# A two-layer encoder: who stores the inverse blocks, when the keys are loaded, and where the post-processing of the recurrence stands

## The chip, the cores and the metric

The kernel runs on one core of a Trainium2 chip. The metric is the device time of one execution in microseconds (us), as the median over runs.

## The reference, cut to what matters

The model has two layers over 1024 positions of width 1024, each a mixer and a SwiGLU feed-forward block with RMS norms and residuals. Layer 0 mixes with a chunked gated MLP beside a pooling mixer. Layer 1 mixes with RWKV-7, a recurrence with a delta rule in 16 heads of 64:

```python
def step(state, inp):
    r_t, w_t, k_t, v_t, a_t, b_t = inp
    sa = jnp.einsum('bhvk,bhk->bhv', state, a_t)
    state = (state * w_t[:, :, None, :] + sa[..., None] * b_t[:, :, None, :]
             + v_t[..., None] * k_t[:, :, None, :])
    return state, jnp.einsum('bhvk,bhk->bhv', state, r_t)
...
mean = jnp.mean(y, axis=-1, keepdims=True)
var = jnp.mean(jnp.square(y - mean), axis=-1, keepdims=True)
y = ((y - mean) * lax.rsqrt(var + GN_EPS)).reshape(bsz, seq, d)
y = y * ln_w.astype(f32) + ln_b.astype(f32)
bonus = jnp.sum(rh * kh * r_k.astype(f32), axis=-1, keepdims=True) * vh
y = (y + bonus.reshape(bsz, seq, d)).astype(h.dtype)
return (y * g) @ w_o, v_first
...
def swiglu(hn, w_gate, w_up, w_down):
    return (jax.nn.silu(hn @ w_gate) * (hn @ w_up)) @ w_down
```

Everything is float32.

## The kernel before

The positions are worked in two halves of 512, called half 0 and half 1 (A and B in the tiles of the stream). A float32 product is done as three products of high and low parts (`mm3`, lines 409 to 411); ScalarE makes the high part (`split`, line 159) and VectorE the low one (line 160). A Tile scheduler sets the order of the instructions on each engine, from the order of the code, from `issue_after` (an instruction that has to be issued behind another) and from a simulated timeline. `drive` interleaves two generators: a stream of dense products (`ffn`, a feed-forward block of a half) and the recurrence, by the numbers that each yields.

For each half, `project` computes the projections of the RWKV mixer and stores keys (`ab_d`), values (`v_d`) and gates (`g_d`) in HBM. The recurrence is done in eight chunks of 64 positions; each chunk needs the inverse of a triangular matrix per head, whose 32x32 diagonal blocks are inverted ahead of it, in `project`. This is `invert` (line 1432), run twice for a half: GpSimd clears the tile `xi` (line 1437), VectorE copies the diagonal (line 1438) and does 31 pairs of a product and a sum (lines 1443 and 1448), makes a transposed copy (line 1450), and three transfers store the blocks to `xi_d` (lines 1452 and 1454). The tile has one buffer, so that the clearing of the second inverse waits for the three stores of the first.

`recur` (line 1469) is the recurrence of a half. `load(c)` (line 1504) loads chunk c: keys `ar` from `ab_d`, the blocks `XT` from `xi_d`, the values `uv` from `v_d`, all on SyncE's queue. The start is `load(0)`, then a stream of other loads, then `load(1)`. `gram` makes the first products of a chunk from the keys (`sm<-ar`), which VectorE turns into `gt`; `flip_bk` transposes keys (`sm<-ident,ar`); `below` and `below2` solve with `XT` and `gt`; `own` solves the chunk's own part into `uv`. `burst(c)` is what a chunk does once the state is there: `below2`, `own`, the next chunk's `gram`, the output `yp`, copied to `ysb` by ScalarE, then the next chunk's transposes, the load of the chunk after it, and its `below`.

`post(jj)` is the post-processing of two chunks, in pieces: loads of gates `gch` and values `vch`, statistics (`bn_stats`), the normalisation, and the gain and bonus on `ysb` (lines 1713 and 1714). It is made after each odd burst, and `between` runs one more of its pieces at three places of a burst. `turn_out`, in the even burst, has TensorE transpose `ysb`, VectorE multiply by the gate (`gch`, line 1731) and SyncE store the result to `y_d`.

For half 0 the main program then opens a tile pool `y0` where the recurrence's memory (`wp0`) was and loads `y_d` into the stream tiles `ahi` and `alo` (`open_act`, `take_act`; ScalarE issues the load of `raw`, then splits it), which the output projection reads. Beside it runs the last group of half B's down projection (`steps_b`), whose sums VectorE adds to the residual `h` (line 503).

```python
ps_es = open_psum("psm0", MIXED)
hb_pool, hb_es = open_pool(name="hb1", bufs=1, side="left")
wp, wp_es = open_pool(name="wp0", bufs=1, side="left")
...
drive(ffn(0, 1, nxt["hn"], f, D0P[:3], nd=2), recur(0, wp, in_pieces(hb_pool, 1, h_d[1, 0]), 6.2), 6.2)
wp_es.close()
y, y_es = open_pool(name="y0", bufs=1, side="left")
ys = open_act(("y", 0), y)
between.append(with_first(0))
drive(ffn(0, 1, nxt["hn"], f, D0P[3:], nd=2))
drive(steps_b)
```

Of the kernel before, what the change touches and what calls it, by code (L numbers as in the profile page):

```python
# [16 lines left out]
P = 128  # L17
# [28 lines left out]
def tile_trunk(  # L46
# [29 lines left out]
    def open_pool(**kw):  # L76
        es = ExitStack()
        pl = es.enter_context(tc.tile_pool(reuse_waits="tile", **kw))
        return pl if kw["name"].startswith("wp") else Lines(pl), es
# [301 lines left out]
    def open_psum(name, tags):  # L381
        es = ExitStack()
        pl = es.enter_context(tc.tile_pool(name=name, bufs=1, space=PSUM, reuse_waits="tile"))
        psum["pool"], psum["tags"] = pl, tags
        return es
# [27 lines left out]
    def rsqrt(t):  # L413
        pool.tensor_tensor(out=t, in0=t, in1=mhalf[:, : t.shape[1]], op=ALU.pow)
# [46 lines left out]
        return norm_bcast(norm_sums(h))  # L461

    def act_tiles(pool_, n=HT):
        return [pool_.tile([P, KT, n], F32R, tag=t, name=t) for t in ("ahi", "alo")]

    def norm_split(h, c0, pool_, spill=None, b=None):

# [964 lines left out]
    def invert(h, p0, iat, tmp):  # L1432

        x2 = tmp("xi", 1, [P, 32, 2, 32])
        xi = x2[:, :, 1, :]
        xf = x2.rearrange("p i a c -> p (i a c)")
        pool.memset(xf, 0.0)
        dve.tensor_copy(xf[:, 32:2048:65], iat[:, 31, :])
        for j in range(31):
            n = 31 - j  # L1440
            t = tmp("it", 1, [P, 256])[:, : n * (j + 1)].rearrange("p (i c) -> p i c", c=j + 1)
            sh = [P, n, j + 1]
            dve.tensor_tensor(  # L1443
                out=t, in0=bc(iat[:, j, j + 1 : 32].unsqueeze(2), sh), in1=bc(xi[:, j, 0 : j + 1].unsqueeze(1), sh),
                op=ALU.mult,
            )
            xs = xi[:, j + 1 : 32, 0 : j + 1]
            dve.tensor_tensor(out=xs, in0=xs, in1=t, op=ALU.add)
            yield
        dve.tensor_copy(x2[:, :, 0, :], xi.rearrange("p i c -> p c i"))  # L1450
        to = xi_d[h][p0 : p0 + 4].rearrange("p r c q i x -> (p r c) q i x")
        sp.dma_start(to[:, 0, :, 0:64], x2[0:64].rearrange("s i a j -> s i (a j)"))
        for q in range(2):
            sp.dma_start(to[:, q, :, 64 - 32 * q : 96 - 32 * q], x2[64:128, :, 0, :])  # L1454

# [11 lines left out]
    def recur(h, wp, stream, ratio):  # L1469
# [5 lines left out]
        def wt(tag, bufs, shape):  # L1475
            return wp.tile(shape, F32, tag=tag, bufs=bufs, name=tag)
# [27 lines left out]
        def load(c):  # L1504
            ab = wt("ar", 2, [P, 2, 8, 2, 64])
            sp.dma_start(ab, ab_d[h][c])
            ar, bk = ab[:, 0], ab[:, 1]
            XT = wt("XT", 2, [P, 8, 96])
            for r in range(2):
                sp.dma_start(XT[rows[r]], xi_d[h][:, r ^ (c % 2), c].rearrange("p q i x -> (q i) p x"))  # L1510
            uv = wt("uv", 2, [P, 2, 8, 64])
            vs = v_d[h][c * 64 : c * 64 + 64]
            sp.dma_start(uv[64:128, 0], vs[:, 0])
            loaded[0] = sp.dma_start(uv[0:64, 1], vs[:, 1])
            gt = wt("gt", 2, [P, 8, 2, P])
            C[c] = (ar, bk, uv, gt, XT)

        def gram(c, q):
            ar, bk, _, gt, _ = C[c]
# [69 lines left out]
        def burst(c, bkt, w1):  # L1589

            ar, _, uv, gt, XT = C[c]
            cg, S0, more = h * 8 + c, S[0], c < 7
            below2(c, w1)
            between()
            Q = own(c, S0)
            between()
            yield 0.1
            if more:
                gram(c + 1, 0)
                between()  # L1600
                yield 0.1
            ou = smt()
            yp = psum["pool"].tile([P, 8, 64], F32, tag="y", bufs=1, name="yp")
            for p in range(8):
                for r in range(2):
                    mm(ou[rows[r], p, :], XT[rows[r], p, 0:64], Q[rows[r], p, :], start=True, stop=True)
                    mm(
                        yp[rows[1 - r], p, :], ar[rows[r], p, 1, :], S0[rows[r], p, :], start=p == 0, stop=False,
                        skip_group_check=True,
                    )  # L1610
            act.activation(uv[rows[0], 0], ou[rows[0]], AF.Copy)
            chain[0] = dve.tensor_copy(uv[rows[1], 1], ou[rows[1]]).ins
            between()
            yield 0.1
            if more:
                gram(c + 1, 1)
                between()
                yield 0.1
            if cg < NCH - 1:
                Sn = wt("S", 2, [P, 8, 64])  # L1620
                os_ = smt()
                each(os_, lambda r, p: bkt[:, p, r * 64 : r * 64 + 64], lambda r, p: uv[:, r, p, :])
                tS = wt("Q", 1, [P, 8, 64])
                dve.tensor_tensor(out=tS, in0=S0, in1=os_, op=ALU.add)
                chain[0] = dve.tensor_tensor(out=Sn, in0=tS, in1=bc(pct[:, cg, :].unsqueeze(2), [P, 8, 64]), op=ALU.mult)
                chain[0] = chain[0].ins
                S[0] = Sn
                between()
                if c == 7:
                    sp.dma_start(state_d, Sn)  # L1630
                yield 0.1
            for p in range(8):
                for r in range(2):
                    mm(
                        yp[rows[1 - r], p, :], gt[:, p, r, 64:128], uv[:, r, p, :], start=False, stop=p == 7,
                        skip_group_check=True,
                    )
            ysb = wt("ysb", 3, [P, 8, 64])
            act.activation(ysb, yp, AF.Copy)
            ypair.append(ysb)  # L1640
            C.pop(c)
            yield 0.1
            if more:
                bkt = flip_bk(c + 1)
                if turned or pieces:
                    for _ in pieces.pop():
                        pass
                    turned.pop()()
                if c < 6:
                    load(c + 2)  # L1650
                if c == 0:
                    with tc.issue_after(loaded[0].ins):
                        for r in range(2):
                            i = sp.dma_start(
                                lnw[rows[1 - r]],
                                rwkv_ln_w[0].rearrange("(p r d) -> r p d", r=2, d=64)[r].partition_broadcast(64),
                            )
                    loaded.append(i)
                yield 0.1
                w1 = below(c + 1)  # L1660
                yield 0.1
            return bkt, w1

        turned, chain, pieces = [], [None], []

        def between():
            if pieces:
                with tc.issue_after(chain[0]):
                    next(pieces[0], None)

        def post(jj):
            ysb = [ypair.pop(0) for _ in range(2)]
            j = h * 4 + jj
            gch = wt("gch", 1, [P, 8, P])
            vch = wt("vch", 1, [P, 2, 8, 64])
# [10 lines left out]
            st = wt("st", 1, [P, 2, 8, 6])  # L1686
            yield
            for r in range(2):
                for p in range(8):
                    dve.bn_stats(out=st[:, r, p, :], in_=ysb[r][:, p, :])  # L1690
                yield
# [7 lines left out]
            dve.tensor_tensor(out=var, in0=var, in1=dm, op=ALU.add)  # L1699
            dve.tensor_scalar(out=var, in0=var, scalar1=1.0 / 64, scalar2=GN_EPS, op0=ALU.mult, op1=ALU.add)  # L1700
            rsqrt(var)
            yield
            dve.scalar_tensor_tensor(out=mean, in0=mean, scalar=-0.5, in1=var, op0=ALU.mult, op1=ALU.mult)
            vb, mb = (bc(t[:, 0:8].unsqueeze(2), [P, 8, 64]) for t in (var, mean))
# [36 lines left out]
        with tc.issue_after(loaded[0].ins):  # L1741
            stream_loaded = stream()
        with tc.issue_after(stream_loaded):
            load(1)
        yield START * ratio
        last.append(newest[0])
# [5 lines left out]
        w1 = below(0)  # L1752
        yield 2.0
        for c in range(8):
            bkt, w1 = yield from burst(c, bkt, w1)
            yield BURST / 2
            if c % 2 == 1:
                pieces[:] = [post(c // 2)]
                next(pieces[0])
            yield BURST / 2  # L1760
        for _ in pieces[0]:
            yield 0.3
        turned.pop()()
# [223 lines left out]


    ps_es = open_psum("psm0", MIXED)
    hb_pool, hb_es = open_pool(name="hb1", bufs=1, side="left")  # L1990
    wp, wp_es = open_pool(name="wp0", bufs=1, side="left")
    f, f_es = open_pool(name="ffn1", bufs=1, side="right")
# [5 lines left out]
    drive(ffn(0, 1, nxt["hn"], f, D0P[:3], nd=2), recur(0, wp, in_pieces(hb_pool, 1, h_d[1, 0]), 6.2), 6.2)  # L1998
    wp_es.close()
    y, y_es = open_pool(name="y0", bufs=1, side="left")  # L2000
    ys = open_act(("y", 0), y)
    between.append(with_first(0))
    drive(ffn(0, 1, nxt["hn"], f, D0P[3:], nd=2))
    drive(steps_b)
# [26 lines left out]
        yield from ffn(1, 0, hnA, f, G1A[0], nd=2, after=spill_a)  # L2031

    def norm_a():
        hnA.extend(norm_split(0, C_FFN + 8, y, n_d[1], norm_bcast(sums)))

    beside(1, blocks(), [1] * 8 + weights_of(G1A[0]), parts, (8, norm_a))
    for e in (f_es, y_es, hb_es, ps_es):
        e.close()
    ps_es = open_psum("psp1", PROJ)
    project(1, hn1, kp, ring, keep, early("n1", "act2", nxt["a_es"]))  # L2040
# [70 lines left out]
```

## Time and profile before

| | before |
|---|---|
| median of 3 runs | 2402.95 us (2401.16 to 2412.61) |
| profiled execution, its own time | 2407.23 us |
| its span | 2405.5 us |
| TensorE busy | 2319.2 us, 96% |
| VectorE, ScalarE, GpSimd busy | 1464.6, 946.9, 171.2 us |
| granted TensorE clock, mean | 0.986 |

The profiled execution is one run, with a profiler on; its span runs from the first to the last instruction. PE is TensorE's matrix products, PEld its weight loads, DVE VectorE, ACT ScalarE, POOL GpSimd, SP SyncE, and SPq or ACTq the issue of a DMA on that engine's queue. A row of waits gives total us, number and longest. A row of a timeline gives start, length, engine, line, operation, the tile written and those read, and in brackets how long the engine had been idle and what ended it. Line numbers are those of the kernel before, unless the text says otherwise. Half 0's recurrence begins near 1043 us and ends near 1240, half 1's runs from about 1600 to 1790.

### The profile page before, as it was taken

Reading aid. Unit: us, or ns where it says so; the run is one execution under the profiler, and the core shown is the slowest. Engines: PE = TensorE matmul, PEld = TensorE weight load, DVE = VectorE, ACT = ScalarE, POOL = GpSimd, SP = SyncE. Lnnn points to the kernel's source line nnn. Section 1 sums busy time; section 2 is a strip of 40 time slices with the busy share of each in tenths; the row PEclk is TensorE's granted clock in tenths of the full one; section 3 lists DMA queues with packets and bytes.
Section 4 is the critical chain, followed back from the end, with each engine's and each line's share of the span. In section 5 each row is a group of like instructions: output and inputs, shape, how many; then the busy total and the mean of one; then the engine's idle time right before and its main releaser. Section 6 shows DMA issues by size and latency. Waiting matters only on the chain.

```text
span 2405.5 us, 37578 instructions
## 1 busy us (share of the span) xinstructions
PE 2319.2 (96%) x15315; PEld 1893.9 (79%) x15315; DVE 1464.6 (61%) x2312; ACT 946.9 (39%) x1467; POOL 171.2 (7%) x195
## 2 busy tenths in 40 slices
PE   8999999999999999889899999998999999999998
PEld 6888888888888788667777777777778788888886
DVE  6445775665568858656768958765664546444443
ACT  6233444444224755323336665423332225222223
POOL 0200000000000022101100022101010001000001
PEclk9999999999999999999999999999999999999999
DMA  5114472334765565775445475776534433433231
GB/s 181 53 49 145 149 198 83 129 99 146 283 226 191 156 173 140 209 218 157 130 135 165 148 199 147 193 222 177 163 89 149 123 88 119 127 96 97 79 114 44
DMA packets 446157, 347.97 MB, mean 145 GB/s; under 512 B 119776, under 2 KB 393312, under 8 KB 443680
## 3 DMA queue, kind: packets, MB, share of 16 engines
q10 hardware_dynamic: 266048, 195.33, 27.3%
q1 hardware_dynamic: 179936, 150.25, 20.9%
q8 instruction: 120, 1.97, 0.4%
q14 instruction: 53, 0.43, 0.1%
HBM read 266.47 MB, written 79.04 MB: 144 GB/s over the span
## 4 chain that ended last, share of the span: by engine, by line
PE 77%; DVE 9%; DMA 6%; issue 2%; ACT 2%; SPq 2%; POOL 2%; ACTq 0%; POOLq 0%; DVEq 0%
PE mm L409 17%; PE mm L410 17%; PE mm L411 17%; PE mm L740 5%; PE mm L742 5%; PE mm L741 5%; PE sm L1491 3%; DMA ar<-ab_d 1%; DVE wlo L160 1%; DMA raw<-y_d 1%; SPq L1454 1%; DVE it L1443 1%; DMA raw<-in_ffn_w_down_dram 1%; PE mm L590 1%; PE mm L591 1%
## 5 line engine op out<-in xcount | busy, mean ns | idle before, releaser
L409 PE MATMUL mm<-ahi,whi 128*128 128x512 f32 x1376 | 541.0, 394 | 4.2 <-ACT ahi L159 2.6
L410 PE MATMUL mm<-alo,whi 128*128 128x512 f32 x1376 | 542.0, 394 | 0.9 <-DVE alo L160 0.9
L411 PE MATMUL mm<-ahi,wlo 128*128 128x512 f32 x1376 | 540.6, 393 | 1.6 <-DVE wlo L160 1.6
L159 ACT ACTIVATE whi<-raw 128x1024 fp32r<-128x1024 f32 (+2 forms) x284 | 286.3, 1014 | 507.1 <-PE mm L410 367.7
L160 DVE TENSOR_TENSOR wlo<-raw,whi 128x1024 fp32r<-128x1024 f32 (+2 forms) x284 | 337.6, 1192 | 233.6 <-ACT whi L159 212.4
L409 PEld LDWEIGHTS mm<-ahi,whi 128*128 128x128 f32 x1376 | 259.0, 188 | 62.9 <-issue 3.5
L411 PEld LDWEIGHTS mm<-ahi,wlo 128*128 128x128 f32 x1376 | 259.2, 188 | 58.5 <-DVE wlo L160 2.9
L410 PEld LDWEIGHTS mm<-alo,whi 128*128 128x128 f32 x1376 | 259.3, 188 | 57.4 <-issue 2.9
L503 DVE TENSOR_TENSOR h<-h,mm 128x512 f32<-128x512 f32 x276 | 185.9, 684 | 156.1 <-PE mm L411 152.9
L411 PE MATMUL mm<-hidhi,wdlo 128*128 128x512 f32 x304 | 119.6, 394 | 0.0
L409 PE MATMUL mm<-hidhi,wdhi 128*128 128x512 f32 x304 | 117.2, 392 | 2.3 <-ACT sg L957 2.3
L410 PE MATMUL mm<-hidlo,wdhi 128*128 128x512 f32 x304 | 118.6, 390 | 0.0
L740 PE MATMUL mm<-ahi,whi 128*128 128x512 f32 x296 | 115.6, 390 | 0.0
L741 PE MATMUL mm<-alo,whi 128*128 128x512 f32 x296 | 115.2, 389 | 0.0
L742 PE MATMUL mm<-ahi,wlo 128*128 128x512 f32 x296 | 113.6, 389 | 0.0
L965 DVE TENSOR_TENSOR sg<-sg,mm 128x512 f32<-128x512 f32 x52 | 35.7, 686 | 125.7 <-PE mm L411 125.7
L159 ACT ACTIVATE wdhi<-raw 128x1024 fp32r<-128x1024 f32 x42 | 43.6, 1058 | 169.0 <-PE mm L410 126.9
L160 DVE TENSOR_TENSOR wdlo<-raw,wdhi 128x1024 fp32r<-128x1024 f32 x42 | 51.4, 1223 | 30.9 <-ACT wdhi L159 29.2
L409 PEld LDWEIGHTS mm<-hidhi,wdhi 128*128 128x128 f32 x304 | 57.2, 188 | 14.7 <-ACT sg L957 2.7
L411 PEld LDWEIGHTS mm<-hidhi,wdlo 128*128 128x128 f32 x304 | 57.2, 188 | 12.2 <-issue 0.5
L410 PEld LDWEIGHTS mm<-hidlo,wdhi 128*128 128x128 f32 x304 | 57.2, 188 | 12.0 <-issue 0.2
L409 PE MATMUL mm<-xhi,whi 128*128 128x512 f32 (+1 forms) x160 | 64.9, 406 | 0.0
(392 smaller groups left out, 4226.2 us busy)
## 6 DMA issues: line engine op xcount, KB each, us to landing
raw<-in_ffn_w_down_dram ACTq DMA_DIRECT2D x88, 512.0 KB
raw<-in_ffn_w_gate_dram ACTq DMA_DIRECT2D x74, 512.0 KB
raw<-in_ffn_w_up_dram ACTq DMA_DIRECT2D x74, 512.0 KB
hid_d<-hid SPq DMA_DIRECT2D x36, 512.0 KB
ar<-ab_d SPq DMA_DIRECT2D x16, 1024.0 KB
hd<-hid_d SPq DMA_DIRECT2D x26, 512.0 KB
raw<-in_ab_w_in_dram ACTq DMA_DIRECT2D x16, 512.0 KB
raw<-in_ab_w_out_dram ACTq DMA_DIRECT2D x16, 512.0 KB
```

The lines of the kernel that those rows point to most:

```text
L159: act.activation(hi, src, AF.Copy)
L160: (eng or dve).tensor_tensor(out=lo, in0=src, in1=hi.bitcast(F32), op=ALU.subtract)
L409: pe.matmul(o, whi, xhi, start=first, stop=False)
L410: pe.matmul(o, whi, xlo, start=False, stop=False)
L411: newest[0] = pe.matmul(o, wlo, xhi, start=False, stop=last).ins
L503: dve.tensor_tensor(out=H[h][:, m, :], in0=H[h][:, m, :], in1=o, op=ALU.add)
L590: pe.matmul(ops[j], xhi[:, k, sl], whi[:, kk], start=(k == 0), stop=False)
L740: pe.matmul(o, wh[:, k, :], x[0][:, k, :], start=st, stop=False, skip_group_check=True)
L741: pe.matmul(o, wh[:, k, :], x[1][:, k, :], start=False, stop=False, skip_group_check=True)
L742: pe.matmul(o, wl[:, k, :], x[0][:, k, :], start=False, stop=k == 3, skip_group_check=True)
L965: dve.tensor_tensor(out=s, in0=s, in1=o, op=ALU.mult)
L1491: i = f(*args, **kw)
```

## The change

The three stores of an inverse go from SyncE's to GpSimd's queue. `load` no longer loads `XT` for chunk 0; a new `load_x(0)` does it behind the stream's loads, so keys and values are issued first. `post` is begun ahead of the odd burst and takes each `ysb` when its statistics are due; `between` may run one piece of it in the odd burst and any number in the even one, and an extra empty `yield` shifts the normalisation by one place. The stream tile `ahi` of half 0's output gets a pool of its own (`y0hi`), outside the recurrence's memory; `alo` stays.

```diff
     def act_tiles(pool_, n=HT):
-        return [pool_.tile([P, KT, n], F32R, tag=t, name=t) for t in ("ahi", "alo")]
+        return [(pool_[i] if type(pool_) is tuple else pool_).tile([P, KT, n], F32R, tag=t, name=t) for i, t in enumerate(("ahi", "alo"))]
...
         to = xi_d[h][p0 : p0 + 4].rearrange("p r c q i x -> (p r c) q i x")
-        sp.dma_start(to[:, 0, :, 0:64], x2[0:64].rearrange("s i a j -> s i (a j)"))
+        pool.dma_start(to[:, 0, :, 0:64], x2[0:64].rearrange("s i a j -> s i (a j)"))
         for q in range(2):
-            sp.dma_start(to[:, q, :, 64 - 32 * q : 96 - 32 * q], x2[64:128, :, 0, :])
+            pool.dma_start(to[:, q, :, 64 - 32 * q : 96 - 32 * q], x2[64:128, :, 0, :])
...
             ar, bk = ab[:, 0], ab[:, 1]
-            XT = wt("XT", 2, [P, 8, 96])
-            for r in range(2):
-                sp.dma_start(XT[rows[r]], xi_d[h][:, r ^ (c % 2), c].rearrange("p q i x -> (q i) p x"))
             uv = wt("uv", 2, [P, 2, 8, 64])
             vs = v_d[h][c * 64 : c * 64 + 64]
             sp.dma_start(uv[64:128, 0], vs[:, 0])
             loaded[0] = sp.dma_start(uv[0:64, 1], vs[:, 1])
-            gt = wt("gt", 2, [P, 8, 2, P])
-            C[c] = (ar, bk, uv, gt, XT)
+            C[c] = (ar, bk, uv, wt("gt", 2, [P, 8, 2, P]), wt("XT", 2, [P, 8, 96]))
+            if c:
+                load_x(c)
+
+        def load_x(c):
+            for r in range(2):
+                loaded[0] = sp.dma_start(C[c][4][rows[r]], xi_d[h][:, r ^ (c % 2), c].rearrange("p q i x -> (q i) p x"))
...
                 bkt = flip_bk(c + 1)
-                if turned or pieces:
-                    for _ in pieces.pop():
-                        pass
+                if c and c % 2 == 0:
+                    exhaust(pieces.pop())
                     turned.pop()()
...
-        turned, chain, pieces = [], [None], []
+        turned, chain, pieces, open_ = [], [None], [], [0]
 
         def between():
-            if pieces:
+            if pieces and open_[0]:
+                open_[0] -= 1
                 with tc.issue_after(chain[0]):
                     next(pieces[0], None)
 
         def post(jj):
-            ysb = [ypair.pop(0) for _ in range(2)]
+            ysb = []
...
             for r in range(2):
+                ysb.append(ypair.pop(0))
                 for p in range(8):
...
             rsqrt(var)
+            yield
             yield
...
             stream_loaded = stream()
         with tc.issue_after(stream_loaded):
+            load_x(0)
+        with tc.issue_after(loaded[0].ins):
             load(1)
...
         for c in range(8):
-            bkt, w1 = yield from burst(c, bkt, w1)
-            yield BURST / 2
             if c % 2 == 1:
                 pieces[:] = [post(c // 2)]
                 next(pieces[0])
-            yield BURST / 2
+            open_[0] = (99, 1)[c % 2]
+            bkt, w1 = yield from burst(c, bkt, w1)
+            yield BURST
...
+    yhi, yhi_es = open_pool(name="y0hi", bufs=1, side="left")
...
-    ys = open_act(("y", 0), y)
+    ys = open_act(("y", 0), (yhi, y))
...
-        hnA.extend(norm_split(0, C_FFN + 8, y, n_d[1], norm_bcast(sums)))
+        hnA.extend(norm_split(0, C_FFN + 8, (yhi, y), n_d[1], norm_bcast(sums)))
```

Since a scheduler sets the order, the following rows show it, in the order of issue on one engine: line, operation, the tile written and those read, shape, number.

SyncE at the start of half 0's recurrence, before, from the last v_d store on (`waits` names what the transfer waits for: DMAHW a transfer of SyncE or ScalarE, DMASW one of GpSimd, PE, DVE or Pool an engine):

```order
L1425 DMA v_d_1976<-epx 256x1x256 [waits DMAHW4_49,Activation_49]
L1452 DMA xi_d_1982<-xi 64x32x64 [waits DMAHW1_49,DVE_49,Pool_49]
L1454 DMA xi_d_1982<-xi 64x32x32 [waits DMAHW2_49]
L1454 DMA xi_d_1982<-xi 64x32x32 [waits DMAHW3_49]
L1506 DMA ar<-ab_d_1974 128x2048 [waits DMAHW5_49,PE_49]
L1510 DMA XT<-xi_d_1982 64x8x96 [waits DMAHW4_49,DMAHW3_49,DMAHW6_49,DMAHW2_49,DMAHW1_49]
```

After (with the new kernel's line numbers; `h` is the stream of half B's residual):

```order
L1425 DMA v_d_1976<-epx 256x1x256 [waits DMAHW1_49,Activation_49]
L1506 DMA ar<-ab_d_1974 128x2048 [waits DMAHW3_49,DMAHW2_49,DMAHW6_49,DMAHW1_49,DMAHW0_49]
L1510 DMA uv<-v_d_1976 64x512 [waits PE_49]
L1511 DMA uv<-v_d_1976 64x512 [waits DMAHW2_49]
L1848 DMA h<-h_d_86 128x1024 [waits DMAHW4_49,DMAHW3_49,PE_49]
L1518 DMA XT<-xi_d_1982 64x8x96 [waits DMASW3_49,DMASW4_49,DMASW2_49,DMASW5_49,DMASW1_49,DMAHW7_49,DMASW0_49,PE_49]
```

The keys no longer stand behind stores of an inverse; `XT` waits for all six of GpSimd.

TensorE at the same place, before (`hidhi` and `whi` are a dense product of half B's feed-forward block):

```order
L409 MATMUL mm<-hidhi,whi 128x512
L410 MATMUL mm<-hidlo,whi 128x512
L411 MATMUL mm<-hidhi,wlo 128x512
L1491 MATMUL sm<-ar 64x128 x32
L1491 MATMUL sm<-ident,ar 128x128 x8
L1491 MATMUL sm<-XT,gt 32x32 x16
```

After:

```order
L411 MATMUL mm<-hidhi,wlo 128x512
L1491 MATMUL sm<-ar 64x128 x32
L409 MATMUL mm<-hidhi,whi 128x512
L1491 MATMUL sm<-ident,ar 128x128 x8
L410 MATMUL mm<-hidlo,whi 128x512
L411 MATMUL mm<-hidhi,wlo 128x512
```

One dense product stands ahead of the transposes now, and 15 between them and the first use of `XT`; before, none. In half 1 there are 46 dense products from the first keys' product to the first use of `XT`, where there were 29.

GpSimd's queue at the two inverses of half 0, after (before, the first rows are followed by the MEMSET alone):

```order
L1374 TENSOR_SCALAR ar<-kkn 128x8 [waits PE_49,Activation_49]
L1377 TENSOR_TENSOR kkn<-kkn,av 128x512 [waits DMAHW1_49,DMAHW2_49,DMAHW0_49,DMAHW7_49,DVE_49,Pool_49]
L1452 DMA xi_d_1982<-xi 64x32x64 [waits DVE_49]
L1454 DMA xi_d_1982<-xi 64x32x32 x2
L1437 MEMSET xi 128x2048 [waits DMASW2_49,DMASW1_49,DMASW0_49]
L1452 DMA xi_d_1982<-xi 64x32x64 [waits DVE_49,Pool_49]
L1454 DMA xi_d_1982<-xi 64x32x32 x2
L1485 MEMSET S 128x512 [waits DMAHW7_49,DMAHW0_49,Activation_49]
```

The stores stand around the memset of the second inverse, which waits for the first three of them.

ScalarE at the end of half 0's recurrence, before (`ysb` is the last block, `raw<-y_d` the load for the output projection):

```order
L1706 ACTIVATE ysb<-ysb,mean,var 128x64 x8
L123 DMA raw<-in_rwkv_w_o_dram 64x4x128 x3
L159 ACTIVATE whi<-raw 128x1024
L968 ACTIVATE hidhi<-sg 128x512
L123 DMA raw<-y_d_82 128x1024
L159 ACTIVATE ahi<-raw 128x1024
```

After:

```order
L1710 ACTIVATE ysb<-ysb,mean,var 128x64 x8
L159 ACTIVATE whi<-raw 128x1024
L419 ACTIVATE nacc<-h 128x512
L422 ACTIVATE nsq<-h 128x512 x5
L123 DMA raw<-y_d_82 128x1024 x3
L422 ACTIVATE nsq<-h 128x512 x2
L159 ACTIVATE ahi<-raw 128x1024 x2
```

The load of the output stands behind squares of half B's residual (`nacc`, `nsq`), and thus at the end of its down projection. On TensorE the last transposes of `ysb` are followed by 84 dense products of half B before the output projection begins, and by 18 after the change.

More of the change, by code (lines that the diff above doesn't have):

```diff
@@ L2033, in norm_a @@
     def norm_a():
-        hnA.extend(norm_split(0, C_FFN + 8, y, n_d[1], norm_bcast(sums)))
+        hnA.extend(norm_split(0, C_FFN + 8, (yhi, y), n_d[1], norm_bcast(sums)))
     beside(1, blocks(), [1] * 8 + weights_of(G1A[0]), parts, (8, norm_a))
-    for e in (f_es, y_es, hb_es, ps_es):
+    for e in (f_es, y_es, hb_es, yhi_es, ps_es):
         e.close()
```

## The prediction

> **What bounds the kernel now.** I read the page first, for the busiest engine, and then the list of what that engine waited for.
>
> ```profile
> PE 2319.2 (96%) x15315; PEld 1893.9 (79%) x15315; DVE 1464.6 (61%) x2312; ACT 946.9 (39%) x1467; POOL 171.2 (7%) x195
> ```
> ```profile
> PE sm L1491 <- DMA ar<-ab_d: 12.8, 3, 9.5
> ```
>
> TensorE works for 96% of the span, and the change removes no matrix product. It can only win or lose idle time of TensorE, plus what a lowered clock costs behind such a pause. The largest single group of waits is for the keys `ar`, 12.8 us in three waits. The chain that ended last shows how the first of them comes about, at the start of half 0's recurrence:
>
> ```profile
> 1035.34 1.11 DVE xi L1450
> ...
> 1036.50 0.61 SPq L1452
> ...
> 1037.16 2.63 SPq L1454
> ...
> 1039.84 4.50 SPq L1454
> ...
> 1044.43 7.93 DMA ar<-ab_d
> ```
>
> The same chain at the start of half 1:
>
> ```profile
> 1592.46 9.81 DMA ar<-ab_d
> 1602.32 3.04 PE sm L1491 x64
> ```
>
> TensorE's timeline says how long it stood:
>
> ```profile
> 1052.41 3.69 PE L1491 MATMUL sm<-ar 64*64 64x128 f32 x64 [9.50 <-DMA ar<-ab_d]
> ```
>
> The keys themselves had been in HBM for long. What delays them is SyncE's queue, in which the three stores of the second inverse stand ahead of them (SyncE's timeline):
>
> ```profile
> 979.23 0.62 SPq L1452 DMA_DIRECT2D xi_d<-xi  x1
> 979.89 11.28 SPq L1454 DMA_DIRECT2D xi_d<-xi  x2
> 991.27 2.42 SPq L1274 DMA_DIRECT2D iat<-at_d  x1
> ...
> 1017.73 0.84 SPq L1425 DMA_DIRECT2D v_d<-epx  x1
> ```
>
> **A. Keys ahead, half 0.** SyncE's last work before the recurrence is now the v_d store, over at 1018.6. The keys are issued there and have 24 us before TensorE wants them at 1042.9 (1052.41 less 9.50). The first wait goes: -9.5 us. The 64 products took 3.69 us here and 3.04 us in half 1, and the windows show why:
>
> ```profile
> 979.00:991.00 12.00, 10.56 (x47) 8.41 (x46) 3.53 (x3) 2.61 (x3) 0.00 (x0) 1.00 0.92 241
> 991.00:1000.00 9.00, 9.00 (x41) 7.42 (x41) 1.38 (x2) 2.52 (x4) 1.15 (x1) 1.00 1.01 246
> ...
> 1036.00:1049.00 13.00, 6.90 (x31) 5.39 (x29) 3.99 (x5) 2.74 (x4) 0.00 (x0) 0.91 0.97 223
> 1049.00:1060.00 11.00, 7.07 (x201) 6.35 (x201) 4.78 (x9) 1.79 (x5) 0.00 (x0) 0.64 1.04 346
> ...
> 1585.00:1598.00 13.00, 13.00 (x59) 10.78 (x58) 6.56 (x8) 4.80 (x7) 0.00 (x0) 1.00 0.94 200
> ```
>
> Columns after the length are busy PE, PEld, DVE, ACT, POOL, then granted clock, DMA share and GB/s. Behind the pause the clock was 0.64. Taking 3.04/3.69 for the 7.07 us of work there, no pause gives -1.3 us.
>
> **B. Keys ahead, half 1.** Of the 12.8 us, 2.7 us is the third wait (the two others are 9.5 and, inside half 0's recurrence, 0.6). It goes too: -2.7 us.
>
> **C. Post-processing a burst sooner.** What TensorE waits for inside the two recurrences, first half 0, then half 1:
>
> ```profile
> PE sm L1491 <- DVE ysb L1714: 2.5, 3, 1.2
> PE sm L1491 <- DVE gt L1530: 2.2, 2, 1.9
> PE sm L1491 <- ACT uv L1611: 2.1, 2, 1.3
> PE yp L1491 <- issue: 2.1, 1, 2.1
> PE sm L1491 <- DVE uv L1612: 1.0, 2, 0.8
> ```
> ```profile
> PE sm L1491 <- DVE gt L1530: 4.0, 2, 3.7
> PE sm L1491 <- ACT uv L1611: 3.4, 2, 2.4
> PE sm L1491 <- DVE ysb L1714: 2.0, 2, 1.0
> ...
> PE sm L1491 <- DVE uv L1612: 0.3, 1, 0.3
> ```
>
> Post-processing ends in `ysb`, whose transposes stay in the even burst while its pieces begin earlier; that should end the 2.5 + 2.0 us of `ysb`. The normalisation now stands behind VectorE's copy of `uv`, worth the 1.0 + 0.3 us. Together -5.8 us. Nothing excludes that VectorE merely delays `gt` elsewhere, so the ends are 0 and, if ScalarE's `uv` (2.1 + 3.4) goes as well, -11.3 us.
>
> **D. The end of half 0.** The order now puts TensorE's transposes of the last block further back among the dense products: 18 products of half B's down projection follow them, where 84 followed, and then comes the output projection. Before, that distance hid a chain from VectorE through HBM back to SBUF:
>
> ```profile
> 1240.18 2.08 DVE gch L1731 x8
> 1242.28 3.46 DMA y_d<-gch
> ...
> 1245.82 3.82 DMA raw<-y_d
> ```
> ```profile
> 1249.66 1.06 ACT L159 ACTIVATE ahi<-raw 128x1024 fp32r<-128x1024 f32 x1 [11.68 <-DMA raw<-y_d]
> ```
> ```profile
> 1250.76 1.23 DVE L160 TENSOR_TENSOR alo<-raw,ahi 128x1024 fp32r<-128x1024 f32 x1 [1.36 <-ACT ahi L159]
> ```
> ```profile
> 1234.96 0.23 PE mm L409
> ```
>
> The chain is 2.1 + 3.5 + 3.8 + 1.1 + 1.2 = 11.7 us; the cover is 18 x 0.23 = 4.1 us. So 7.6 us is uncovered, and I add 1.4 us (six products' worth) because the first output block wants four such pieces one after the other: +9.0 us. Waits that stand there already go into this one:
>
> ```profile
> PE mm L409 <- DVE h L503: 2.9, 3, 1.2
> ```
>
> With them the net is +6.1 us. Ends: 0, if the other pieces of the order hold TensorE back anyway, and +11.7 us, the whole chain. Moving `ahi` out of the recurrence's memory lets its first write happen sooner, but the chain and not the memory is what ends last, so I give it nothing.
>
> **E. GpSimd's stores.** The trace holds no DMA issued by GpSimd, so their time is unknown. From SyncE, store 1 took from 979.23 to at latest the memset that waits for it; the second inverse's VectorE work starts soon behind:
>
> ```profile
> 998.85 1.82 POOL L1437 MEMSET xi<- 128x2048 f32 x1 [30.89 <-DMA v_d<-sg]
> ```
> ```profile
> 1002.70 0.19 DVE L1438 COPY xi<-iat 128x32 f32<-128x32 f32 x1
> ```
> ```profile
> 1530.07 0.61 SPq L1452 DMA_DIRECT2D xi_d<-xi  x1
> ```
> ```profile
> 1546.30 0.19 DVE L1438 COPY xi<-iat 128x32 f32<-128x32 f32 x1
> ```
> ```profile
> L1454 SPq DMA_DIRECT2D xi_d<-xi x8: 1616/3446/9188, 979.9 to 1587.9; - x8
> ```
>
> Store 1 is thus 19.6 us, and store 2, from 1036.5 to the end of that window at 1049, 12.5 us. The DMA engines' share there is 0.92 to 1.01 whoever issues, so the lower end is these same times. For the upper end I take three issues at SyncE's slowest, 9.19 us each, plus 2 us to land: 30 us. I take the measured times, since the share names the DMA engines as the limit. Where this is hidden: store 1 has until about 21.7 us (memset done 1.8 us behind it, and the copy at 1002.70 behind that) before VectorE stands at the copy, with the weight splits for TensorE queued behind it. Store 2 must be in before `XT` is read. TensorE would start the keys' products at 1042.9, take 3.04 us, then 8 transposes (1.3 us, an estimate) and 16 dense products of 0.23 us: 1050.9. Store 2 at 1049.0 and the `XT` load, 2.5 to 3.8 us (below the load of 512 KB above), gives 1051.5 to 1052.8. The second inverse's input is no longer queued behind 11.28 us of stores, which may give up to 2 us back. I take +1.0 us. In half 1, 46 dense products (10.6 us) stand between keys and `XT`, so nothing is late there at these times. SyncE's other loads move only up; GpSimd's own operations behind the stores are two memsets.
>
> **Sum.** -9.5 - 1.3 - 2.7 - 5.8 + 6.1 + 1.0 = -12.2 us. The profiled execution took 2407.2 us, 4.3 us over the median of the runs; the same step from the median 2402.95 gives 2390.7, say 2390.5 us. That sits at the edge of what counts as a change here: 0.5%, or 12 us, about what a measurement of this kernel can tell from none.
>
> A rule speaks against E. The Trainium skill's page "SBUF — State Buffer", section "SBUF: two separate sides", says that a GpSimd DMA has its descriptors written by GpSimd's own cores, and that these are locked out of a shared port while VectorE runs certain copies. The rows above show VectorE busy 4.9 us of store 1 and 4.0 us of store 2, so by a full lock the stores would be 24.5 and 16.5 us, E about +8 instead of +1, and the time some 2398 us. No trace here shows such a store; the windows' mostly idle VectorE is why I don't take it.
>
> **The rivals.** (1) *GpSimd's stores are slow: slower.* Price by size X per store: half 0 loses X - 21.7 at the memset and X - 12 at `XT`; half 1 loses about X - 16 at its memset (its copy at 1546.30 stood 16.2 us behind the store's start at 1530.07). At X = 22 us that is 0.3 + 10 + 6, which cancels the gain; at 25 us, 3.3 + 13 + 9 = 25 us, or 2415; at 30 us, 8.3 + 18 + 14 = 40 us less E's 1, which makes 2430. For it: 6144 short runs per inverse that a core must describe, and the row L1454's spread. Against it: DMA engines already full. (2) *The gain is given back: same.* C brings nothing and D costs its whole 11.7 less 2.9: -9.5 - 1.3 - 2.7 + 8.8 + 1 = -3.7, 2399. For it: VectorE's order has to take `gt` from somewhere. (3) *`XT` takes the keys' place: same.* Inverse, store and `XT` remain one chain, and half of A (5 us) comes back as a wait for `XT`; 2396. The skill's "DMA: Bandwidth & Descriptors", section "Issuing engines are not separate DMA queues", would have it that another issuer saves only issue time; in rows, that is this case. (4) *More is gained:* C at -11.3 and D at 0: 2407 would lose 24 us; 2379.
>
> **How the numbers follow.** Forecast 0.46 (own range 2384 to 2396; half of it below 2391), rivals 2 and 3 together 0.22, rival 4 0.14, rival 1 0.18. Of rival 1, some 0.03 ends within 0.5%. Faster: 0.24 + 0.14 + 0.02 = 0.40; same: 0.22 + 0.20 + 0.03 = 0.45; slower 0.15. The range leaves out the extreme of rival 4 (0.05) and the part of rival 1 beyond 2420 (0.10): 2377 to 2420.
>
> **What would show it.** A: no wait of `sm` for `ar`, keys issued near 1019, clock near 1.0 at 1049. B: none at 1600. C: `ysb` and VectorE's `uv` gone from the waits. D: a TensorE pause of 6 to 9 us before the output projection of half 0, released by ScalarE's `ahi`. E: the second memset within 2 us of 999, and `XT` read by 1053; a memset at 1005 or a wait on `XT` above 5 us would show the slow stores and make the forecast wrong, as would a D above 12 us.

## The result: 0.57% faster, near the forecast, with errors in its terms that offset each other

| | before | after |
|---|---|---|
| median of 11 runs | 2404.07 us (2396.93 to 2412.61) | 2390.36 us (2381.92 to 2399.13) |
| ratio after to before | | 0.9943, 95% interval 0.9928 to 0.9959 |
| profiled execution | 2407.23 us | 2399.13 us |
| its span | 2405.5 us | 2397.4 us |
| TensorE busy | 2319.2 us | 2316.8 us |

The forecast was 2390.5 us. The profiled execution of after is the slowest of its eleven runs, so the pair of profiles differs by 8.1 us only; one run of `best`, below, took 5361.78 us for a reason not known and stands outside its ratio. I compare the profiles stage by stage. A second profile of the changed kernel is among the experiments (span 2385.5 us).

What TensorE waited for in the changed kernel, whole run:

```profile
PE mm L409 <- ACT ahi L159: 11.4, 2, 9.8
...
PE sm L1491 <- DVE gt L1532: 6.0, 4, 3.0
PE mm L409 <- DVE h L503: 5.7, 3, 4.5
PE sm L1491 <- DVE ysb L1718: 3.8, 4, 1.2
PE mm L411 <- DVE wlo L160: 3.1, 2, 2.6
PE sm L1491 <- DMA XT<-xi_d: 2.7, 1, 2.7
```

The keys are gone from the list. In their place stand a pause of 9.8 us for `ahi`, one of 2.7 us for `XT` (4.1 us in the second profile), and one of 4.5 us for `h`. GpSimd's timeline shows its stores (the second row holds two), and the memset that waits for the first three:

```profile
977.29 1.32 POOL L1452 DMA_DIRECT2D xi_d<-xi  x1 [11.61 <-DVE xi L1450]
978.62 2.17 POOL L1454 DMA_DIRECT2D xi_d<-xi  x2
989.22 1.82 POOL L1437 MEMSET xi<- 128x2048 f32 x1 [8.42 <-DMA xi_d<-xi]
1028.67 1.09 POOL L1452 DMA_DIRECT2D xi_d<-xi  x1 [37.63 <-DVE xi L1450]
```

Store 1 is over 11.9 us after its start (12.9 us in the second profile); from SyncE it had been 19.6 us. The second inverse is ready to store at 1028.67, where it was 1036.50. SyncE's queue beside it (L1848 are the loads of half B's residual `h`, L1518 those of `XT`):

```profile
1011.69 0.32 SPq L1506 DMA_DIRECT2D ar<-ab_d  x1
...
1021.71 20.42 SPq L1848 DMA_DIRECT2D h<-h_d  x4
1043.37 1.29 SPq L1518 DMA_DIRECT2D XT<-xi_d  x2
```

and TensorE's start of half 0's recurrence:

```profile
1038.93 1.98 PE L1491 MATMUL sm<-ar 64*64 64x128 f32 x64
1041.18 1.03 PE L1491 MATMUL sm<-ident,ar 128*128 128x128 f32 x8
...
1048.35 0.45 PE L1491 MATMUL sm<-XT,gt 32*32 32x32 f32 x32 [2.69 <-DMA XT<-xi_d]
```

The keys were issued at 1011.7 and their products began without a wait at 1038.9; the 64 products took 1.98 us instead of 3.69. The end of half 0 is the chain of work there, in order of time:

```profile
1232.54 2.08 DVE gch L1735 x8
1234.63 3.53 DMA y_d<-gch
1238.24 6.14 DMA raw<-y_d
1244.48 1.06 ACT ahi L159
```

with TensorE waiting at its end, and again twice for the next block's weights:

```profile
1245.59 0.80 PE L409 MATMUL mm<-ahi,whi 128*128 128x512 f32 x1 [9.83 <-ACT ahi L159]
1257.77 0.50 PE L409 MATMUL mm<-ahi,whi 128*128 128x512 f32 x1 [1.42 <-ACT whi L159]
1261.08 0.50 PE L411 MATMUL mm<-ahi,wlo 128*128 128x512 f32 x1 [2.57 <-DVE wlo L160]
```

Adding up TensorE's idle time by stage, from the instruction records of the traces, gives the balance (us; "projections" runs from the first transposes of a half's projections to its first keys' product, "end" from the last transposes of `ysb` in half 0 to half 1's projections):

| idle TensorE in | before | after | after, second profile |
|---|---|---|---|
| all up to half 0's projections | 11.5 | 12.5 | 12.5 |
| half 0's projections, to the keys | 20.5 | 8.1 | 4.9 |
| half 0's recurrence | 11.6 | 6.9 | 7.9 |
| end of half 0 | 11.4 | 19.8 | 18.8 |
| half 1's projections, to the keys | 8.1 | 5.2 | 6.5 |
| half 1's recurrence | 11.2 | 16.1 | 12.0 |
| the rest | 2.3 | 2.5 | 1.6 |
| sum | 76.7 | 71.1 | 64.1 |

So 12 to 16 us are won ahead of the keys and 4 to 5 in half 0's recurrence (the wait for `XT` included), and 7 to 8 are given back at its end. Half 1's recurrence has 1 to 5 us more idle time than before.

### The profile page after: what moved, and what is told of

It reads as the page before. It is cut to its first block, busy times and chain, and to the rows that moved or that the text cites. A ratio compares the mean times of both kernels' runs of the same rounds, so it can differ in the third digit from the quotient of the medians.

```text
span 2397.4 us, 37575 instructions
## 1 busy us (share of the span) xinstructions
PE 2316.8 (97%) x15315; PEld 1895.5 (79%) x15315; DVE 1466.6 (61%) x2312; ACT 947.1 (40%) x1467; POOL 183.9 (8%) x207
## 3 DMA queue, kind: packets, MB, share of 16 engines
q0 software_dynamic: 1216, 4.20, 0.7%
## 4 chain that ended last, share of the span: by engine, by line
PE 80%; DVE 8%; DMA 6%; issue 2%; ACT 2%; POOL 1%; SPq 0%; ACTq 0%; POOLq 0%; DVEq 0%
PE mm L409 18%; PE mm L410 18%; PE mm L411 18%; PE mm L740 5%; PE mm L742 5%; PE mm L741 5%; PE sm L1491 4%; DVE wlo L160 1%; DVE it L1443 1%; DMA raw<-in_ffn_w_down_dram 1%; ACT whi L159 1%; PE yp L1491 1%; DMA raw<-y_d 1%; DVE xi L1448 1%; DMA raw<-in_rwkv_w_k_dram 1%
## 5 line engine op out<-in xcount | busy, mean ns | idle before, releaser
L409 PE MATMUL mm<-ahi,whi 128*128 128x512 f32 x1376 | 543.6, 396 | 13.0 <-ACT ahi L159 11.4
L409 PEld LDWEIGHTS mm<-ahi,whi 128*128 128x128 f32 x1376 | 260.0, 189 | 71.7 <-ACT ahi L159 12.6
L160 DVE TENSOR_TENSOR wdlo<-raw,wdhi 128x1024 fp32r<-128x1024 f32 x42 | 53.0, 1262 | 27.1 <-ACT wdhi L159 27.1
L740 PEld LDWEIGHTS mm<-ahi,whi 128*128 128x128 f32 x296 | 55.6, 188 | 11.7 <-issue 0.2
```

The costliest lines, as they stand in the source:

```text
L160: (eng or dve).tensor_tensor(out=lo, in0=src, in1=hi.bitcast(F32), op=ALU.subtract)
L409: pe.matmul(o, whi, xhi, start=first, stop=False)
L740: pe.matmul(o, wh[:, k, :], x[0][:, k, :], start=st, stop=False, skip_group_check=True)
```

## The experiments

Each ratio is to the kernel before on the same chip, with its 95% interval.

**Which part of the change does it.** Three kernels, each with one part undone or done alone. `sp_store` is the changed kernel with the stores back on SyncE:

```diff
-        pool.dma_start(to[:, 0, :, 0:64], x2[0:64].rearrange("s i a j -> s i (a j)"))
+        sp.dma_start(to[:, 0, :, 0:64], x2[0:64].rearrange("s i a j -> s i (a j)"))
...
-            pool.dma_start(to[:, q, :, 64 - 32 * q : 96 - 32 * q], x2[64:128, :, 0, :])
+            sp.dma_start(to[:, q, :, 64 - 32 * q : 96 - 32 * q], x2[64:128, :, 0, :])
```

> The changed kernel with the three stores of each inverse back on SyncE; keys first, post-processing and tiles as changed. Theory S (the stores' queue is the cause): the order puts the keys behind the stores on SyncE again, so a wait of about 9 us for the keys returns at 1043, and of the 13.7 us gained some 10 are lost: about 2400 us. Theory K (splitting keys from XT and the earlier post-processing bring most of it): the wait is for ar only as long as the stores, but the products between keys and XT and the earlier post-processing keep over half of the gain: 2396 us or less.

Measured: 2400.61 us, ratio 0.9988 (0.9975 to 1.0001). The wait for the keys is back at its full size:

```profile
1050.98 2.41 PE L1491 MATMUL sm<-ar 64*64 64x128 f32 x40 [9.49 <-DMA ar<-ab_d]
```

As theory S had it: without the stores' move, loading keys ahead of `XT` gains nothing, since on SyncE both stand behind the stores. The interval of this kernel includes no change at all.

`pool_only` is the kernel before with only these three lines on GpSimd (the same lines of the diff the other way round).

> The kernel before with nothing but the stores of the inverses issued by GpSimd; XT is still loaded with the keys. Theory S: store 1 lands about 12 us after its start, the second inverse ends some 6 us earlier, the keys wait for nothing: 2391 us (within 3 us of the changed kernel), and the pause at the end of half 0 of some 13 us is there as well. Theory K: only the first wait goes, the waits inside the recurrences stay: 2397 us.

Measured: 2405.69 us, ratio 1.0003 (0.9989 to 1.0017): nothing, and both theories missed. Its trace shows a new wait:

```profile
1044.25 0.79 PE L409 MATMUL mm<-hidhi,whi 128*128 128x512 f32 x1 [7.14 <-DVE h L503]
```

```profile
1035.63 1.29 SPq L1510 DMA_DIRECT2D XT<-xi_d  x2
1037.02 0.58 SPq L1513 DMA_DIRECT2D uv<-v_d  x1
1037.65 0.59 SPq L1514 DMA_DIRECT2D uv<-v_d  x1
1038.34 1.95 SPq L1842 DMA_DIRECT2D h<-h_d  x4
```

The keys come in time, but `XT`, which waits for GpSimd's stores, now stands at the head of SyncE's queue, with the four loads of `h` behind it. They are issued at 1038.3, VectorE's sums into `h` wait for them, and TensorE waits 7.14 us for VectorE. By the stages of the table, this kernel has 15.4 us less idle time ahead of half 0's keys than the kernel before, and more everywhere behind: 3.7 us in half 0's recurrence (with the 7.14), 5.7 at its end, where the pause for `ahi` is 9.6 us, and 4.9 in half 1's recurrence. So nothing is left of the gain, and the wait for `h` is a large part of that but not all of it. The split of `load` matters here for another transfer than I had in mind: it is `h` that has to get past `XT`.

`old_post` is the changed kernel with the post-processing of before:

```diff
-                if c and c % 2 == 0:
-                    exhaust(pieces.pop())
-                    turned.pop()()
+                if turned or pieces:
+                    for _ in pieces.pop():
+                        pass
+                    turned.pop()()
...
-            if c % 2 == 1:
-                pieces[:] = [post(c // 2)]
-                next(pieces[0])
-            open_[0] = (99, 1)[c % 2]
             bkt, w1 = yield from burst(c, bkt, w1)
-            yield BURST
+            yield BURST / 2
+            if c % 2 == 1:
+                pieces[:] = [post(c // 2)]
+                next(pieces[0])
+            yield BURST / 2
```

(with the extra `yield`, the late taking of `ysb` and the condition in `between` undone as well).

> The changed kernel with the post-processing of before (begun after the odd burst, normalisation one place earlier). The prediction's term C: 5.8 us are lost, 2396 us, with waits of sm for ysb and for VectorE's uv of 4 to 6 us. Theory S: the waits inside half 0's recurrence went because of the stores, not of the post-processing; 2390 us within 3, and half 0's waits as in the changed kernel.

Measured: 2395.92 us, ratio 0.9971 (0.9955 to 0.9987). Its median is 5.6 us above the changed kernel's, but the two intervals just overlap. What TensorE waits for in its half 0's recurrence (1050 to 1236 us), and then in the changed kernel's:

```profile
PE sm L1491 <- DVE ysb L1716: 3.1, 4, 1.2
PE sm L1491 <- DVE gt L1532: 1.9, 1, 1.9
PE sm L1491 <- DVE uv L1614: 1.2, 3, 0.8
```
```profile
PE sm L1491 <- DVE ysb L1718: 1.4, 2, 1.0
PE sm L1491 <- DVE uv L1614: 0.7, 3, 0.3
```

`gt` is in the first list alone. In half 0's recurrence, without the wait for `XT`, the traces have 7.4 us of idle time with the old post-processing and 4.2 with the new (3.8 in the second profile), so some 3.5 of the 5.6 us are found there; where the others are is not shown. Stores and split together make 0.29%, and the earlier post-processing about as much again, with the uncertainty of these intervals.

**What the end of half 0 costs.** `cover` moves 48 products (two blocks of hidden units of half B's down projection) from beside the projections to the end of the recurrence:

```diff
-    D0B = [[a, a + 1, a + 2] for a in range(f, f + 12, 3)], [[a, a + 1] for a in range(f + 12, 22, 2)]
+    D0B = [[f, f + 1, f + 2], [f + 3, f + 4, f + 5], [f + 6, f + 7], [f + 8, f + 9]], [[f + 10, f + 11], [f + 12, f + 13]]
...
-    third = {g[2] for g in D0B[0]}
+    third = {g[2] for g in D0B[0] if len(g) > 2}
```

> The changed kernel with 48 dense products of half B's down projection (two blocks of hidden units) done at the end of half 0's recurrence instead of beside the projections; the order then puts some 86 products behind the last transposes where 18 stood. Theory G (the gain is given back at the end of half 0, because the products that covered the chain through y_d have been used up): the pause of 13.8 us there falls to 2 to 4 us, 2381 us. Rival M (the products hide as much where they stood before): the pause goes but the projections stage waits as much longer, 2388 to 2392 us.

Measured: 2381.41 us, ratio 0.9910 (0.9890 to 0.9930), the time of theory G. The wait for `ahi` before half 0's output projection is gone, but others stand in its place; of waits from 1218 to 1290 us its trace has

```profile
PE mm L409 <- DVE h L503: 6.0, 3, 3.9
PE mm L409 <- DMA hd<-hid_d: 3.0, 1, 3.0
```

So the waits there did not fall to 2 to 4 us. By the stages of the table, idle time at the end of half 0 is 16.3 us (16.9 in the repetition `cover_again` below), where it was 19.8 and 18.8. The larger fall stands elsewhere, in half 1's recurrence: 3.1 and 7.2 us, where it was 16.1 and 12.0. What TensorE waits for there, in the changed kernel and then in `cover`:

```profile
PE sm L1491 <- DVE gt L1532: 6.0, 4, 3.0
...
PE sm L1491 <- DVE ysb L1718: 2.5, 2, 1.2
```
```profile
PE sm L1491 <- DVE gt L1532: 1.3, 1, 1.3
```

The edit does not touch that stage, but the scheduler's order has changed in it too: 510 dense products stand between its first keys' product and its last transposes of `ysb`, where 459 stood. Theory G thus has the time right and the place only in part, and the new order in half 1 is a rival that no run here excludes.

The chain through `y_d` takes as long as in the kernel before (its load of `raw` is issued alone again), and now runs beside products:

```profile
1223.57 3.49 DMA y_d<-gch
...
1227.13 3.79 DMA raw<-y_d
...
1231.02 1.07 ACT ahi L159
```

Repeated with the changed kernel on one chip (`cover_again`, `after_again`):

> The kernel of cover once more, on the same chip as the two others of this call: 2381 us within 4 if the first result holds.

> The changed kernel itself, on the same chip as cover: 2390 us within 4; a profile with a pause before half 0's output projection of 9 to 10 us, and none for the keys.

Measured: `cover_again` 2380.80 us, ratio 0.9928 (0.9909 to 0.9948); `after_again` 2388.34 us, ratio 0.9943 (0.9922 to 0.9964). The medians stand 9.0 and 7.5 us apart in the two comparisons. The intervals overlap in both, in the first by a hair, and the two profiles taken with the second comparison have nearly the same idle time, 63.4 us for `cover_again` and 64.1, so the size of the gain is uncertain. The same move in the kernel before, `cover_b`:

> The kernel before with the same 48 dense products moved to the end of half 0's recurrence. Theory G (the products are missing there only after the change): before, the pauses there add up to 3.4 us, so at most these go: 2399 to 2403 us. Rival M (moving products there is a gain of its own, for example because the projections stage gets shorter without loss): the 9 us that it brought to the changed kernel come here too, 2394 us.

Measured: 2414.86 us, ratio 1.0052 (1.0039 to 1.0066). It is no gain of its own, which speaks against rival M, but theory G did not expect a loss of 12 us either. The move has a price (in the trace of `cover_b` a new wait of 3.0 us for the hidden units read back, idle time of 80.7 us against 76.7, and 2327.1 us of busy TensorE against 2319.2 at a mean clock of 0.983). Where all of the price lies, and why the same move gains in the changed kernel, I have not settled.

**Trying to better it.** `best` adds a third buffer for those hidden units and loads chunk 0's `XT` on GpSimd's queue:

```diff
-                loaded[0] = sp.dma_start(C[c][4][rows[r]], xi_d[h][:, r ^ (c % 2), c].rearrange("p q i x -> (q i) p x"))
+                loaded[0] = (sp if c else pool).dma_start(C[c][4][rows[r]], xi_d[h][:, r ^ (c % 2), c].rearrange("p q i x -> (q i) p x"))
...
-    _, hslot = slots_of(f, 0, 2)
+    _, hslot = slots_of(f, 0, 3)
```

> The changed kernel with the 48 products moved as in cover, a third buffer for the hidden units read back there, and chunk 0's XT loaded on GpSimd's queue, behind the stores, instead of SyncE's. Theory Q (XT is late because SyncE's queue stands at the loads of h until 1042, and not because of the store, which landed at 1041.0): the wait for XT of 2.7 us falls below 1, the wait for the hidden units of 3.0 us goes, 2377 us. Rival R (XT is bound by the store and the full DMA engines): the XT wait stays at 2 to 3 us, 2380 us.

Measured: 2392.74 us, ratio 0.9953 (0.9939 to 0.9967). Theory Q falls, and so does R:

```profile
1045.91 0.65 PE L1491 MATMUL sm<-XT,gt 32*32 32x32 f32 x32 [8.73 <-DMA XT<-xi_d]
```
```profile
XT<-xi_d POOLq DMA_DIRECT2D x4, 192.0 KB, 8.2
```

GpSimd issued the two loads at 1037.1, 0.6 us after the store had landed, and they took 5.6 and 8.0 us to land (the median of the program's four is 8.2). In `cover` SyncE had issued them at 1033.9, 3.2 us after the store, and `XT` was there 4.9 us later. `cover_nh3` keeps the third buffer and puts `XT` back on SyncE:

> The kernel of cover with a third buffer for the hidden units read back, and XT on SyncE's queue as in the changed kernel. If the loss of best came from XT's load on GpSimd's queue (8.7 us of waiting for XT there, 2.75 in cover): the XT wait is back below 4 us, the wait for the hidden units of 3.0 us is gone, 2379 us. If it came from the buffer or the order that it brings: 2388 us or more, as best.

Measured: 2390.47 us, ratio 0.9963 (0.9949 to 0.9977). Its wait for `XT` is 2.9 us and that for the hidden units is gone, but its trace has new ones, of 3.7 us for the next chunk's keys and 3.4 us for `h`. So most of the loss of `best` against `cover` comes with the buffer and the order that it brings. Its trace does not show how: its idle time adds up to 62.2 us, where the two of `cover` have 61.7 and 63.4. `cover` is the fastest version I found.

**The remaining parts.** `old_yhi` puts the high stream tile back (`open_act(("y", 0), y)`, and no `y0hi`):

> The changed kernel with half 0's high stream tile back in the recurrence's memory. TensorE's order is the same. The prediction (the tile's place brings nothing, the chain through y_d ends last): 2390 us within 2. Rival T (the tile's memory is what the load's split waits for): the pause before the output projection grows from 9.8 to 12 us or more, 2393 us.

Measured: 2390.13 us, ratio 0.9950 (0.9931 to 0.9969): no effect. `copies` tests the rule that VectorE's copies hold up GpSimd's transfers:

```diff
             pool.dma_start(to[:, q, :, 64 - 32 * q : 96 - 32 * q], x2[64:128, :, 0, :])
+        for i in range(32):
+            dve.tensor_copy(tmp("it", 1, [P, 256]), xf[:, i % 8 * 256 : i % 8 * 256 + 256])
```

> The changed kernel with 32 additional VectorE copies of 128x256 f32 from SBUF to SBUF behind each inverse, so that they run while GpSimd issues its stores; their results are used by nothing. Rule L (such copies keep GpSimd from writing descriptors): the three transfers, which land 6.4 to 10.9 us behind their issue, take at least the copies' 8 to 10 us longer, 16 us or more, and the issues themselves exceed 1.1 us. Rival N (nothing is locked here): landing in 6 to 11 us as before; the kernel gets longer only by VectorE's own time, 10 to 30 us.

Measured (one run): 2399.85 us. VectorE copied throughout the second store:

```profile
1036.23 10.79 DVE L1456 COPY it<-xi 128x256 f32<-128x256 f32 x29
```

and the transfers' median times to land, in the changed kernel and then with the copies, are

```profile
xi_d<-xi POOLq DMA_DIRECT2D x4, 512.0 KB, 6.7
xi_d<-xi POOLq DMA_DIRECT2D x8, 256.0 KB, 9.7
```
```profile
xi_d<-xi POOLq DMA_DIRECT2D x4, 512.0 KB, 8.2
xi_d<-xi POOLq DMA_DIRECT2D x8, 256.0 KB, 10.5
```

They are 1.5 and 0.8 us longer, not 8 to 10, and the issues stay at 1.1 to 1.3 us. The time, 9.5 us above the changed kernel's median, is at the edge of rival N's range. VectorE's added work has a part in it: the memset of the second inverse waits for the copies until 999.7 us, where it was 989.2. But the two engines are not indifferent to each other. Of the 128 copies, most of 0.29 us, eight that ran beside the issue of a store took 0.59 to 0.86 us, and one beside a memset of GpSimd 0.57 us. There it was VectorE that was held up.

## Why the prediction came out right

**A (-9.5 and -1.3 us): right.** The keys' wait went entirely. The idle time ahead of the keys fell by 12.4 us, more than the term, since some of the shorter waits there went as well. The clock in the stretch behind, granted 0.64 before, is 0.91:

```profile
1041.00:1052.00 11.00, 8.31 (x66) 6.57 (x67) 4.83 (x8) 1.36 (x3) 0.00 (x0) 0.91 0.84 228
```

In the second profile, behind its longer wait for `XT`, it is 0.72 from 1040 to 1052 us, so the 1.3 us are not reliably won. What the term did not see is that the split of `load` is needed for `h`, as `pool_only` shows.

**B (-2.7 us): not reliably there.** The keys' wait in half 1 went. But there the loads of `h` wait for GpSimd's stores (presumably for the memory that these still read), and in the profile of after they bring a wait of 4.5 us; the chain of work shows them:

```profile
1578.29 9.15 DMA xi_d<-xi
...
1587.71 5.43 DMA h<-h_d
...
1593.27 0.70 DVE h L503
```

In the second profile of the same kernel no wait over 0.9 us stands there. The prediction had called nothing late in half 1, because it looked only at `XT`.

**C (-5.8 us): the size near, the rows not.** `old_post` is 5.6 us slower. But `ysb`, which was to lose all of its 4.5 us, still has 3.8 us in the whole run; a good part of the gain is `gt` and `uv` in half 0. In half 1 the idle time of the recurrence did not fall at all (11.2 before, 12.0 and 16.1 after): waits for `gt` rose there from 4.0 to 6.0 us (6.9 in the second profile), as the term had allowed for. That the size comes out near is luck to that extent.

**D (+6.1 us): right in kind, too small.** The pause is 9.8 us, with 4.0 us for weights behind it: 13.8, against the 9.0 of the term. Net, the stage has 8.4 us more idle time than before (7.4 in the second profile), against 6.1. Two parts were mis-sized. The load of `raw`, taken as 3.8 us from a row in which it was issued alone, took 6.1 us (5.2 in the second profile) with three issued together. And where the term has 1.4 us for further pieces, TensorE waited 4.0 us for weights. The clock behind the pause is left out altogether, although A counts it: from 1232 to 1262 us it was granted 0.77, where it had been 1.00, and the mean clock of the two profiles is the same, 0.986. `cover`, with 86 products in place of 18, has no pause for `ahi` there, so the pause is a matter of cover; its gain in time does not come from that place alone.

**E (+1.0 us): too small, and for another reason.** The stores were bounded from below by SyncE's times, on the ground that the DMA engines were full whoever issues. Store 1 took 11.9 us (12.9 in the second profile) instead of 19.6, at full DMA engines:

```profile
977.30:989.10 11.80, 11.80 (x58) 9.88 (x57) 5.35 (x7) 4.83 (x7) 3.49 (x3) 1.00 1.05 324
```

The share is as before, but 324 GB/s were moved where it had been 241 and 246. Together with the second inverse's input, no longer queued, the second store began 7.8 us earlier, and it landed at 1041.0 instead of the 1049.0 of the term. `XT` was late all the same, by 2.7 us and in the second profile by 4.1, since SyncE's queue stood at the loads of `h` until 1042.1: it issued `XT` 2.4 and 3.9 us after the store had landed. This is read from the two traces; `best`, which was to test it, changed too much else.

The total fits partly by luck, as idle time by stage shows. Ahead of half 0's keys 3 to 6 us more were won than A has, and in its recurrence 1 to 2 us more than C and E have together. The end of half 0 lost 1 to 2 us more than D's net, and half 1's recurrence lost 1 to 5 us where C has a gain of 2.3. Of the rivals, slow stores (1) did not occur; `XT` in the keys' place (3) is there with 2.7 us (4.1 in the second profile) of its 5; and giving back (2) is half true: D came near its whole chain, but C did bring its gain in half 0. The rule on VectorE's copies, weighed in the prediction at 2398 us, is not borne out for such copies: the stores landed about 1 us later where it asks for 8 to 10. What shows is VectorE held up beside GpSimd's issues, by up to 0.6 us a copy. Whether one long copy would hold up a store for as long as it runs, no run shows.

## What to carry to other kernels

When transfers move to another queue, list everything that stood behind them on the old one and everything that now waits for them: here the move alone was worth nothing, and 0.29% once the loads of `h` had got past `XT`. A wait filled with other work takes that work from somewhere, so look at what it had been covering: the 84 products at the end of half 0 had hidden a chain of 12 us, and with 18 left it came into the open as a pause of 9.8 us. When an edit then removes the pause, add up the idle time of every stage before calling that the cause: `cover` had the forecast time, and most of the idle time that it saved lay in another stage. A time for a transfer from a row where it was issued alone (3.8 us) was too short when the new order issued three at once (5.2 to 6.5 us in three traces), though no run isolates the reason.

## What was not expected of the hardware

GpSimd's stores needed far fewer packets than SyncE's for the same bytes. Before, SyncE's queue, and after, both queues:

```profile
q1 hardware_dynamic: 179936, 150.25, 20.9%
```
```profile
q1 hardware_dynamic: 155168, 146.05, 19.9%
q0 software_dynamic: 1216, 4.20, 0.7%
```

24768 packets became 1216, at 4.2 MB either way, some 170 bytes a packet against 3.5 KB. By the packet records, 16384 packets of 128 bytes and 8192 of 256 became 1024 of 4096; the rest are of 4 bytes. That would account for faster stores at equally full engines, but no run varies the packets alone, and the two stores had different neighbours: the second took some 12 us from either queue. A load of 192 KB issued by GpSimd, on the other hand, took 8.2 us to land.
